# Seven block products for eight in half of the k tiles of two SwiGLU layers' gate and up projections

## The chip, the cores and the metric

The kernel runs on one core of a Trainium2 chip. The metric is the device time of one execution in microseconds (us); the lower, the better. Engines are named as the profile names them: PE is TensorE (PEld its weight loads), DVE is VectorE, ACT is ScalarE, POOL is GpSimd, and SP is the queue from which nearly all DMAs are issued.

## The reference

One decoder layer in float32 on 256 tokens of width 2048: a SwiGLU feed-forward layer at half step, a token mixer, and a second feed-forward layer, each between two RMS norms.

```python
def swiglu(h, w_gate, w_up, w_down):
    return (jax.nn.silu(h @ w_gate) * (h @ w_up)) @ w_down
...
    h = h + 0.5 * rms_norm(swiglu(rms_norm(h, pre1), gate1, up1, down1), post1)
    h = h + rms_norm(hybrid_mixer(rms_norm(h, preM), ...), postM)
    h = h + 0.5 * rms_norm(swiglu(rms_norm(h, pre2), gate2, up2, down2), post2)
```

`w_gate` and `w_up` are 2048 x 5632, `w_down` is 5632 x 2048. The mixer (gated linear attention in four heads, softmax attention in eight) is not changed but for where its constants are loaded.

## The kernel before, in words

**Precision.** Every float32 matmul is made of three matmuls in fp32r: a value is split into a high part (rounded to fp32r) and a low part (the rest), and hi x hi, hi x lo and lo x hi are summed. Activations are split once and kept in `xh` (x, transposed, times the norm's weights: per k tile of 128 rows, 256 columns of high parts and 256 of low parts). The factor 1/rms of each token, `late.rc[t]`, is applied to the product instead of to x.

**Weights.** A weight tile is 128 x 1024: two k tiles of 512 output columns. `order` (L57 to L80) lists all of them in the order of use. `prep` (L86) loads one on SP into one of 4 `raw` buffers, makes `whi` on ACT (L99) and `wlo` on DVE (L100); these have RING = 7 places. `take` and `done` (L118, L126) hand a tile to the matmuls and give it back.

**Up blocks.** `up` (L392) makes 512 of the 5632 columns: `columns` (L274) runs over eight tiles of the gate's weights, then over eight of the up projection's; each tile gives 12 matmuls in `mmt` (L258 to L266: two token tiles of 128, two k tiles, three precision terms), with a slice of `xh` as the stationary tile and 512 columns of the weight tile as the moving one. So a block has 192 matmuls. ACT applies silu to the gate's sums (L399), DVE multiplies by the up sums (L403), and `turned` (L406), a generator whose next piece is run by `step` after each weight tile, transposes the result on PE (L411) and splits it into an `act` tile (L415, L416; four buffers). There are 11 such blocks in each feed-forward layer (FFN 1 and FFN 2).

**Down groups.** `down` (L302) takes two blocks' `act` tiles as k and adds to the four 512-wide column groups of `f`, with the same 12 matmuls per weight tile; the sum is copied (L317) or added (L319) to `f`. Groups and blocks alternate (L427 to L436): four blocks, then a group of 16 tiles and two blocks, and so on. The last group makes the norm's sums as it goes (L333 to L335) and hands over to the next stage.

**PSUM.** `pt` (L190) gives one of four tiles of two banks each, which is all of PSUM.

**Order.** The code is straight-line Python. Buffers are given out and the instructions of each engine are put into a fixed order by the framework's scheduler before the run, by data dependence and program order; so an instruction can run well ahead of its place in the code when its inputs and buffers are free. On the chip each engine then works through its list in order, and waits on semaphores.

**Other loads.** `post_weight` (L184) broadcasts a norm's weights (1 MB) into `wpost` and scales them on ACT (L188); `mixer_constants` (L178) loads the mixer's tables. Both stand in the code between FFN 1's groups. The mixer's low-rank decay weights are one short tile in `order`, spread into ring places with POOL memsets (L104 to L111), and used at L528.

Of the kernel before, what the change touches and what calls it, by code (L numbers as in the profile page):

```python
# [34 lines left out]
RING = 7  # L35
# [7 lines left out]


@with_exitstack
def layer(ctx, tc, xT, x, wn, wpo, cst, msk, bdec, wup, wglr, gu1, dn1, win, wo, gu2, dn2, out):
# [4 lines left out]
    ring = ctx.enter_context(tc.tile_pool(name="ring", bufs=RING))  # L51
# [5 lines left out]
    order = []  # L57

    def plan_down(w, groups):
        n = w.shape[0] // 4  # L60
        for a, b in groups:
            for m in range(4):
                order.extend(w[m * n + i] for i in range(a // 2, b // 2))

    def plan_ffn(gu, dn):
        def up(*blocks):
            for b in blocks:
                order.extend(gu[i] for i in range(b * 16, b * 16 + 16))

        up(0, 1, 2, 3)  # L70
        for g in range(4):
            plan_down(dn, DOWN_FFN[g:g + 1])
            up(*((4, 5), (6, 7), (8, 9), (10,))[g])
        plan_down(dn, DOWN_FFN[4:])

    plan_ffn(gu1, dn1)
    order.extend(win[i] for i in range(24))
    order.append(wglr)
    order.extend(win[i] for i in range(24, 96))
    plan_down(wo, DOWN_MIX)  # L80
    plan_ffn(gu2, dn2)

    ready = []
    used, freed = [0], [0]

    def prep(cuts=1):  # L86
        i = len(ready)
        src = order[i]
        n = src.shape[-1]
        raw = ring.tile([P, 1024], F32, name="raw", bufs=4)  # L90
        w = n // cuts
        for c in range(0, n, w):
            SY.dma_start(raw[:, c:c + w], src[:, c:c + w])
        hi = ring.tile([P, 1024], F32R, name="whi")
        lo = ring.tile([P, 1024], F32R, name="wlo")
        if n == 1024:
            for c in range(0, n, w):
                c = slice(c, c + w)
                A.activation(hi[:, c], raw[:, c], AF.Copy)  # L99
                V.tensor_tensor(lo[:, c], raw[:, c], hi[:, c].bitcast(F32), ALU.subtract)  # L100
            ready.append((hi, lo))
        else:

            r = raw[:, :n].rearrange("p (h k c) -> p h k c", h=2, c=RANK)  # L104
            for half, both in enumerate((hi, lo)):
                nc.gpsimd.memset(both.bitcast(F32), 0.0)
# [6 lines left out]
    def ahead():  # L113

        while len(ready) < min(len(order), freed[0] + RING):
            prep()
# [185 lines left out]
    def down(groups, lhs, fin):  # L302

        ss = [small.tile([P, 4], F32, name="ss%d" % t) for t in range(NT)]
        for g, (a, b) in enumerate(groups):
# [17 lines left out]
            for t in range(NT):  # L323
                for m in range(4):
                    p = pt()[:, t]
                    for i in range(n):
                        if t == 0:
                            slots.append(take())
# [486 lines left out]
```

## Time and profile before

| | us |
|---|---|
| three runs, median | 1931.71 |
| lowest and highest | 1931.46, 1932.37 |
| the profiled execution | 1932.02 |
| its span in the profile | 1930.2 |

The span runs from the first to the last recorded instruction; the profiled execution's own time is 1.8 us longer. Busy times of an engine are the sum of its instructions' durations with overlaps counted once; since matmuls are pipelined, a matmul's own duration (some 393 ns) is longer than the distance between two of them. "Idle before" is the time an engine stood still just ahead of an instruction of that group, and behind the arrow stands what ended it.

### The profile page before, as it was taken

The page shows a single profiled execution, that of the slowest core. Times are in us where ns is not written, and L with a number is a line of the kernel's source. Part 1 is how long each engine was busy: PE and PEld are TensorE (multiplying, and loading weights), DVE is VectorE, ACT ScalarE, POOL GpSimd, SP SyncE. Part 2 cuts the span into 40 slices and gives each one's busy share as a digit, 9 for nine tenths or more (in the row PEclk, how much of TensorE's full clock was granted, in tenths as well). Part 3 has the DMA queues.
Part 4 walks back from the last instruction along what each step waited for, and adds up shares of the span by engine and source line. Part 5 has one row for each costly group of instructions (what it writes and reads, how often), then busy time and mean ns, then how long its engine had stood idle before and what let it go on. Part 6 is the DMA issues. An engine that isn't in the chain of part 4 may idle for free.

```text
span 1930.2 us, 22431 instructions
## 1 busy us (share of the span) xinstructions
PE 1891.8 (98%) x8728; PEld 1562.9 (81%) x8728; DVE 1045.1 (54%) x1141; ACT 884.0 (46%) x1052; POOL 2.0 (0%) x6
## 2 busy tenths in 40 slices
PE   8999999999999998999999998999999999999997
PEld 6888888888888885889888885888888888888885
DVE  5554455545445458468455647544445545545455
ACT  8444444344443436454445547444444344344442
POOL 0000000000000000000000000000000000000000
PEclk9999999999999999999999998999999999999999
DMA  9755555555555554554454554555555555555552
GB/s 326 251 191 188 185 194 185 191 191 185 195 187 186 196 185 142 178 163 144 134 170 159 190 196 133 193 188 190 189 188 193 186 191 186 193 187 189 192 186 87
DMA packets 98650, 356.24 MB, mean 185 GB/s; under 512 B 11088, under 2 KB 11344, under 8 KB 97904
## 3 DMA queue, kind: packets, MB, share of 16 engines
q1 hardware_dynamic: 97968, 353.77, 55.3%
q8 instruction: 68, 1.11, 0.2%
q10 hardware_dynamic: 576, 1.05, 0.2%
q14 instruction: 38, 0.31, 0.0%
HBM read 352.67 MB, written 2.10 MB: 184 GB/s over the span
## 4 chain that ended last, share of the span: by engine, by line
PE 94%; DVE 3%; ACT 1%; DMA 1%; issue 1%; SPq 0%; DVEq 0%; ACTq 0%
PE pt L266 27%; PE pt L264 27%; PE pt L265 27%; PE pt L252 6%; PE pt L253 3%; PE pt L411 1%; DVE wlo L100 1%; PE pt L601 1%; ACT whi L99 1%; DMA raw<-in_gu 0%; DMA h<-in_x 0%; DVE f L335 0%; DVE h L359 0%; DVE f L333 0%; ACT junk L360 0%
## 5 line engine op out<-in xcount | busy, mean ns | idle before, releaser
L100 DVE TENSOR_TENSOR wlo<-raw,whi 128x1024 fp32r<-128x1024 f32 (+1 forms) x657 | 802.9, 1223 | 818.9 <-ACT whi L99 818.0
L99 ACT ACTIVATE whi<-raw 128x1024 fp32r<-128x1024 f32 (+1 forms) x657 | 695.0, 1059 | 962.6 <-PE pt L266 868.9
L264 PE MATMUL pt<-whi,xh 128*128 128x512 f32 x1664 | 654.7, 393 | 11.2 <-ACT whi L99 6.0
L266 PE MATMUL pt<-whi,xh 128*128 128x512 f32 x1664 | 651.5, 392 | 2.1 <-DVE xh L378 2.1
L265 PE MATMUL pt<-wlo,xh 128*128 128x512 f32 x1664 | 650.3, 391 | 0.8 <-DVE wlo L100 0.8
L264 PEld LDWEIGHTS pt<-whi,xh 128*128 128x128 f32 x1664 | 313.7, 189 | 81.6 <-ACT xh L377 11.6
L266 PEld LDWEIGHTS pt<-whi,xh 128*128 128x128 f32 x1664 | 313.7, 189 | 70.1 <-DVE xh L378 5.0
L265 PEld LDWEIGHTS pt<-wlo,xh 128*128 128x128 f32 x1664 | 313.9, 189 | 65.6 <-DVE wlo L100 2.0
L264 PE MATMUL pt<-whi,act 128*128 128x512 f32 x704 | 278.6, 396 | 0.0
L265 PE MATMUL pt<-wlo,act 128*128 128x512 f32 x704 | 277.7, 395 | 0.0
L266 PE MATMUL pt<-whi,act 128*128 128x512 f32 x704 | 277.7, 394 | 0.0
L252 PE MATMUL pt<-xh,whi 128*128 128x512 f32 x512 | 182.0, 399 | 0.0
L266 PEld LDWEIGHTS pt<-whi,act 128*128 128x128 f32 x704 | 132.6, 188 | 30.9
L265 PEld LDWEIGHTS pt<-wlo,act 128*128 128x128 f32 x704 | 132.7, 188 | 30.5
L264 PEld LDWEIGHTS pt<-whi,act 128*128 128x128 f32 x704 | 132.7, 188 | 30.5
L253 PE MATMUL pt<-xh,wlo 128*128 128x256 f32 x512 | 143.6, 281 | 0.0
L252 PEld LDWEIGHTS pt<-xh,whi 128*128 128x128 f32 x512 | 96.1, 188 | 22.7 <-issue 0.8
L253 PEld LDWEIGHTS pt<-xh,wlo 128*128 128x128 f32 x512 | 96.6, 189 | 0.2
L319 DVE TENSOR_TENSOR f<-f,pt 128x1024 f32<-128x1024 f32 x32 | 39.1, 1221 | 20.6 <-PE pt L266 20.6
L403 DVE SCALAR_TENSOR_TENSOR fs<-pt,rs_c,fs 128x512 f32<-128x512 f32 x44 | 31.1, 747 | 10.0 <-PE pt L266 10.0
L399 ACT ACTIVATE fs<-pt,rs_c 128x512 f32<-128x512 f32 x44 | 27.5, 673 | 0.0
L416 DVE TENSOR_TENSOR act<-pt,act 128x1024 fp32r<-128x1024 f32 x22 | 26.8, 1217 | 0.0
(138 smaller groups left out, 529.6 us busy)
## 6 DMA issues: line engine op xcount, KB each, us to landing
raw<-in_gu SPq DMA_DIRECT2D x351, 512.0 KB, 3.3
raw<-in_dn SPq DMA_DIRECT2D x176, 512.0 KB, 3.3
raw<-in_win SPq DMA_DIRECT2D x96, 512.0 KB, 3.3
raw<-in_wo SPq DMA_DIRECT2D x32, 512.0 KB, 3.2
wpost<-in_wpo SPq DMA_DIRECT2D x3, 1024.0 KB, 4.8
hT<-in_xT SPq DMA_DIRECT2D x8, 256.0 KB, 7.1
h<-in_x SPq DMA_DIRECT2D x2, 1024.0 KB, 8.2
out<-h SPq DMA_DIRECT2D x4, 256.0 KB, 2.6
```

The lines of the kernel that those rows point to most:

```text
L99: A.activation(hi[:, c], raw[:, c], AF.Copy)
L100: V.tensor_tensor(lo[:, c], raw[:, c], hi[:, c].bitcast(F32), ALU.subtract)
L252: T.matmul(o, hv[:, k, c], a, start=first and k == 0, stop=False)
L253: T.matmul(o[:, S:], lv[:, k, c], a[:, 0:S], start=False, stop=last and k == 1)
L264: T.matmul(o, hi, hv[:, i], start=first and i == 0, stop=False)
L265: T.matmul(o, hi, lv[:, i], start=False, stop=False)
L266: T.matmul(o, lo, hv[:, i], start=False, stop=last and i == 1)
L319: V.tensor_tensor(f[:, m], f[:, m], p, ALU.add)
L399: A.activation(s[:, t], g2[:, t], AF.Silu, scale=late.rc[t])
L403: V.scalar_tensor_tensor(s[:, t], u2[:, t], late.rc[t], s[:, t], op0=ALU.mult, op1=ALU.mult)
L411: T.transpose(p[:, j // 2, j % 2 * S + t * P:j % 2 * S + (t + 1) * P], s[:, t, j * P:(j + 1) * P], ident)
L416: V.tensor_tensor(a[:, :, S:], src, a[:, :, 0:S].bitcast(F32), ALU.subtract)
```

## The change

In each FFN, block 0 stays as it was. Blocks 1 to 10 become *units*. In a unit, the gate and up projections of 512 columns each are taken together as a 2 x 2 x 2 block product: two token tiles, two halves of k, and two projections. For the first eight of the 16 k tiles this is done by Strassen's algorithm in Winograd's form: four weight tiles W11, W12, W22, W21 (a *quad*; two quads per unit) give seven products with W11, W22, W21 and the sums T1 = W11 + W12, T2 = T1 + W22, T3 = W12 + W22, T4 = T2 + W21. The sums are made on DVE in float32 and split into high and low parts like any weight tile; each of these seven *forms* takes a ring place and is used for six matmuls (one token tile's worth of stationary data, two k tiles, three terms). The other eight weight tiles of a unit are used as before, 12 matmuls each, and add to the same PSUM sums. The unit's order is: quad, four single tiles, quad, four single tiles.

The matching sums of x over token tiles and k halves are made once per FFN (`mixed`, started inside block 0) and kept split in `mix`. As the two token tiles have different 1/rms factors, x of the second tile is scaled by their ratio `rho` (turned into a row by a small matmul) before the sums, and `rho` is applied to the products that need it at the end. Five of the products are combined at the second quad's end (one copy on ACT, four additions on DVE), the rest at the unit's end (four instructions on DVE, one silu of 1024 columns on ACT, one product on DVE). A unit holds all four PSUM tiles.

Around it: RING is 8 instead of 7, and there are 5 `raw` buffers instead of 4. A down group is cut into two halves (two column groups each), and units stand between the halves: block 0, unit 1, unit 2, half, unit 3, half, unit 4, and so on; the last two groups follow unit 10. `act` has 3 buffers instead of 4. `wpost` is no tile of its own any more: in the FFNs it takes the place of `mix` after unit 10, in two loads; in the mixer it takes two of its tiles. The mixer's constants, and the decay weights, are loaded at the start of the mixer into its own pool, which uses the memory of FFN 1's tiles; the decay weights are split by one ACT and one DVE instruction. The squares that went to a `junk` tile go to `f` or to PSUM.

```diff
-RING = 7
+RAW = 5
+RING = 8
+NQ = 2
...
+FFN = [("up", 0, ()), ("up", 1, ()), ("up", 2, ())]
+for _g in range(4):
+    for _i, _ms in enumerate(((0, 1), (2, 3))):
+        FFN += [("down", _g, _ms), ("up", 3 + 2 * _g + _i, ())]
+FFN += [("down", 4, range(4)), ("down", 5, range(4))]
+UNIT = [("q", 0), ("s", 4), ("s", 12), ("s", 5), ("s", 13), ("q", 1), ("s", 6), ("s", 14), ("s", 7), ("s", 15)]
...
+    def plan_quad(w11, w12, w22, w21):
+        forms.extend((kind, len(source)) for kind in ("w11", "t1", "t3", "w22", "t2", "w21", "t4"))
+        source.extend((w11, w12, w22, w21))
...
+    def added(name, a, b):
+        t = sum_pool[0].tile([P, 1024], F32, name=name, tag="sum", bufs=2)
+        V.tensor_tensor(t, a, b, ALU.add)
+        sums.append(t)
...
+        if kind == "w" or kind == "w11":
+            if kind == "w11":
+                added("t1", w[0], w[1])
+            split(w[0], cuts)
+        elif kind == "t1":
+            added("t2", sums[-1], w[2])
+            split(sums[-2])
+        elif kind == "t3":
+            added("t3", w[1], w[2])
+            split(sums[-1])
+        elif kind == "w22":
+            split(w[2])
+        elif kind == "t2":
+            split(sums[-2])
+        elif kind == "w21":
+            V.tensor_tensor(sums[-2], sums[-2], w[3], ALU.add)
+            split(w[3])
        else:
+            split(sums[-2])
...
-                A.activation(junk, c, AF.Square, accum_out=self.hs[t][:, m:m + 1])
+                A.activation(f[:, m, t], c, AF.Square, accum_out=self.hs[t][:, m:m + 1])
...
+            mix = fp.tile([P, 2, 4, 2 * NQ, P], F32R, name="mix", tag="mix")
+            def mixed():
+                while None in late.rc:
+                    yield
+                V.reciprocal(rho, late.rc[0])
+                V.tensor_tensor(rho, rho, late.rc[1], ALU.mult)
+                row = small.tile([P, P], F32, name="rrow", bufs=1)
+                A.activation(row, row_of([rho]), AF.Copy)
+                yield
+                v = f.rearrange("p m t c -> p (m t c)").rearrange("p (k s) -> p k s", s=S)
+                for k in range(0, 4 * NQ, 4):
+                    c = v[:, k:k + 4]
+                    V.tensor_tensor(c, xh[:, k:k + 4, 0:S].bitcast(F32), xh[:, k:k + 4, S:].bitcast(F32), ALU.add)
+                    yield
+                    V.tensor_tensor(c[:, :, P:], c[:, :, P:], row[:, None, :].to_broadcast([P, 4, P]), ALU.mult)
+                    yield
+                k0, k1 = slice(0, 2 * NQ), slice(2 * NQ, 4 * NQ)
+                x11, x12, x21, x22 = v[:, k0, 0:P], v[:, k1, 0:P], v[:, k0, P:], v[:, k1, P:]
+                m = v[:, 4 * NQ:8 * NQ].rearrange("p k s -> p (k s)").rearrange("p (n k s) -> p n k s", n=4, s=P)
+                V.tensor_tensor(m[:, 0], x22, x21, ALU.subtract)
+                V.scalar_tensor_tensor(m[:, 1], m[:, 0], -1.0, x11, op0=ALU.mult, op1=ALU.subtract)
+                yield
+                V.tensor_tensor(m[:, 2], x11, x21, ALU.subtract)
+                V.tensor_tensor(m[:, 3], x12, m[:, 1], ALU.add)
+                for i in range(0, 4, 2):
+                    yield
+                    A.activation(mix[:, 0, i:i + 2], m[:, i:i + 2], AF.Copy)
+                    V.tensor_tensor(mix[:, 1, i:i + 2], m[:, i:i + 2], mix[:, 0, i:i + 2].bitcast(F32), ALU.subtract)
...
+            def product(o, slot, q, lhs, first, last):
+                hv, lv = (x.rearrange("p (k c) -> p k c", k=2) for x in slot)
+                for i in range(2):
+                    a = lhs(2 * q + i)
+                    T.matmul(o, a[:, 0], hv[:, i], start=first and i == 0, stop=False)
+                    T.matmul(o, a[:, 0], lv[:, i], start=False, stop=False)
+                    T.matmul(o, a[:, 1], hv[:, i], start=False, stop=last and i == 1)
+            def unit(b):
+                p16, p57, p23, q4e = pt(), pt(), pt(), pt()
+                into = {"w11": (p16[:, 0], xlhs(0, 0)), "t1": (p57[:, 0], mlhs(0)), "t3": (p57[:, 1], mlhs(2)),
+                        "t2": (p16[:, 1], mlhs(1)), "w22": (p23[:, 1], mlhs(3)), "w21": (p23[:, 0], xlhs(1, 0)),
+                        "t4": (q4e[:, 0], xlhs(1, 1))}
+                s = fp.tile([P, NT, 512], F32, name="fs", bufs=2)
+                u = fp.tile([P, NT, 512], F32, name="fu")
+                nq, ns = 0, 0
+                for kind, i in UNIT:
+                    if kind == "q":
+                        nq += 1
+                        for _ in range(7):
+                            name = forms[used[0]][0]
+                            o, lhs = into[name]
+                            alone = name in ("w11", "t1", "t3", "t2")
+                            product(o, take(), i, lhs, nq == 1, alone and nq == NQ)
+                            done()
+                        if nq == NQ:
+                            A.activation(s[:, 0], p16[:, 0], AF.Copy)
+                            V.tensor_tensor(s[:, 1], p16[:, 1], s[:, 0], ALU.add)
+                            V.tensor_tensor(u[:, 0], p57[:, 0], s[:, 1], ALU.add)
+                            V.tensor_tensor(s[:, 1], p57[:, 1], s[:, 1], ALU.add)
+                            V.tensor_tensor(u[:, 1], p57[:, 1], u[:, 0], ALU.add)
+                    else:
+                        ns += 1
+                        slot = take()
+                        j, k = i // 8, 2 * (i % 8)
+                        end = ns > 2 * (8 - 2 * NQ) - 2
+                        mmt(p23[:, j], 0, slot, (k, k + 1), False, end, xrhs)
+                        mmt(q4e[:, j], 1, slot, (k, k + 1), j == 1 and ns == 2, end, xrhs)
+                        done()
+                        if nq == NQ:
+                            step()
+                V.tensor_tensor(s[:, 0], p23[:, 0], s[:, 0], ALU.add)
+                V.tensor_tensor(u[:, 0], p23[:, 1], u[:, 0], ALU.subtract)
+                V.scalar_tensor_tensor(s[:, 1], q4e[:, 0], rho, s[:, 1], op0=ALU.mult, op1=ALU.add)
+                V.scalar_tensor_tensor(u[:, 1], q4e[:, 1], rho, u[:, 1], op0=ALU.mult, op1=ALU.subtract)
+                A.activation(s, s, AF.Silu, scale=late.rc[0])
+                V.scalar_tensor_tensor(s, u, late.rc[0], s, op0=ALU.mult, op1=ALU.mult)
+                side.append(turned(b, s))
...
-                a = fp.tile([P, 4, 2 * S], F32R, name="act", bufs=4)
+                a = fp.tile([P, 4, 2 * S], F32R, name="act", bufs=3)
...
+            for kind, i, ms in FFN:
+                if kind == "down" and i < 5:
+                    down(DOWN_FFN[i], ms, arhs)
+                elif kind == "down":
+                    down_last(DOWN_FFN[i], arhs, wpost, fin)
+                else:
+                    (up if i == 0 else unit)(i)
+                if kind == "up" and i == 10:
+                    both = fp.tile([P, 2, 4, 2 * NQ, P], F32, name="wpost", tag="mix")
+                    both = both.rearrange("p a b c s -> p (a b c s)")
+                    wpost = [both[:, h * 1024:h * 1024 + 1024].rearrange("p (m c) -> p m c", m=2) for h in range(2)]
+                    for i in range(2):
+                        post_weight(wpost[i], post, scale, i)
...
+        gr = mp.tile([P, KT, RANK], F32, name="gr")
+        gw = mp.tile([P, KT, 2 * RANK], F32R, name="gw")
+        cum, bias = cm[:, 0:128], cm[:, 128:512]
+        SY.dma_start(gr.rearrange("p k c -> p (k c)"), wglr)
+        SY.dma_start(bd, bass.AP(tensor=bdec.tensor, offset=bdec.offset, ap=[[0, P], [1, HG * DK]]))
+        SY.dma_start(wu, wup)
+        SY.dma_start(cm, cst[:, 256:768])
+        SY.dma_start(ms, msk)
...
+        A.activation(gw[:, :, 0:RANK], gr, AF.Copy)
+        V.tensor_tensor(gw[:, :, RANK:], gr, gw[:, :, 0:RANK].bitcast(F32), ALU.subtract)
+        for k in range(KT):
+            T.matmul(p[:2 * RANK], gw[:, k], xh[:, k, :], start=k == 0, stop=k == KT - 1)
```

## Rows read from the trace of the kernel before

**Rows 1.** The page, parts 1 and 2: busy time, and the span in 40 slices.
```profile
PE 1891.8 (98%) x8728; PEld 1562.9 (81%) x8728; DVE 1045.1 (54%) x1141; ACT 884.0 (46%) x1052; POOL 2.0 (0%) x6
...
PEclk9999999999999999999999998999999999999999
```

**Rows 2.** The page, part 4: the chain that ended last, by engine and by line.
```profile
PE 94%; DVE 3%; ACT 1%; DMA 1%; issue 1%; SPq 0%; DVEq 0%; ACTq 0%
PE pt L266 27%; PE pt L264 27%; PE pt L265 27%; PE pt L252 6%; PE pt L253 3%; PE pt L411 1%; DVE wlo L100 1%; PE pt L601 1%; ACT whi L99 1%; DMA raw<-in_gu 0%; DMA h<-in_x 0%; DVE f L335 0%; DVE h L359 0%; DVE f L333 0%; ACT junk L360 0%
```

**Rows 3.** Groups by line: busy us, mean ns | idle us before, releasers.
```profile
L100 DVE TENSOR_TENSOR wlo<-raw,whi 128x1024 fp32r<-128x1024 f32 (+1 forms) x657 | 802.9, 1223 | 818.9 <-ACT whi L99 818.0 <-PE pt L266 0.3
L99 ACT ACTIVATE whi<-raw 128x1024 fp32r<-128x1024 f32 (+1 forms) x657 | 695.0, 1059 | 962.6 <-PE pt L266 868.9 <-PE pt L252 68.5 <-issue 12.3
L264 PE MATMUL pt<-whi,xh 128*128 128x512 f32 x1664 | 654.7, 393 | 11.2 <-ACT whi L99 6.0 <-ACT xh L377 5.2
L266 PE MATMUL pt<-whi,xh 128*128 128x512 f32 x1664 | 651.5, 392 | 2.1 <-DVE xh L378 2.1
L265 PE MATMUL pt<-wlo,xh 128*128 128x512 f32 x1664 | 650.3, 391 | 0.8 <-DVE wlo L100 0.8
...
L264 PE MATMUL pt<-whi,act 128*128 128x512 f32 x704 | 278.6, 396 | 0.0
...
L319 DVE TENSOR_TENSOR f<-f,pt 128x1024 f32<-128x1024 f32 x32 | 39.1, 1221 | 20.6 <-PE pt L266 20.6
L403 DVE SCALAR_TENSOR_TENSOR fs<-pt,rs_c,fs 128x512 f32<-128x512 f32 x44 | 31.1, 747 | 10.0 <-PE pt L266 10.0
L399 ACT ACTIVATE fs<-pt,rs_c 128x512 f32<-128x512 f32 x44 | 27.5, 673 | 0.0
L416 DVE TENSOR_TENSOR act<-pt,act 128x1024 fp32r<-128x1024 f32 x22 | 26.8, 1217 | 0.0
...
L272 DVE TENSOR_TENSOR bt<-pt,tb 128x512 f32<-128x512 f32 x16 | 11.0, 686 | 3.1 <-ACT tb L271 3.1
...
L736 DVE TENSOR_TENSOR go<-go,g 128x1024 f32<-128x1024 f32 x1 | 1.2, 1224 | 1.3 <-ACT g L510 1.3
```

**Rows 4.** The chain in order of time: start us, us, what; the blocks' transposes.
```profile
58.60 0.87 PE pt L411 x8
103.01 0.87 PE pt L411 x8
147.44 0.88 PE pt L411 x8
192.00 0.87 PE pt L411 x8
280.86 0.87 PE pt L411 x8
```

**Rows 5.** Timeline of PE around one block's transposes: start us, us, instruction.
```profile
102.85 1.03 PE L411 MATMUL pt<-cs,fs 128*128 128x128 f32 x8
103.64 0.48 PE L264 MATMUL pt<-whi,xh 128*128 128x512 f32 x1
```

**Rows 6.** Timeline of DVE in three stretches: start us, us, instruction [idle before].
```profile
39.64 0.16 DVE L202 SCALAR_TENSOR_TENSOR rs_c<-rs_a,rs_r 128x1 f32<-128x1 f32 x1
...
53.20 0.75 DVE L403 SCALAR_TENSOR_TENSOR fs<-pt,rs_c,fs 128x512 f32<-128x512 f32 x1 [1.49 <-PE pt L266]
53.86 1.22 DVE L100 TENSOR_TENSOR wlo<-raw,whi 128x1024 fp32r<-128x1024 f32 x1
54.99 0.74 DVE L403 SCALAR_TENSOR_TENSOR fs<-pt,rs_c,fs 128x512 f32<-128x512 f32 x1
55.66 3.49 DVE L100 TENSOR_TENSOR wlo<-raw,whi 128x1024 fp32r<-128x1024 f32 x3
...
97.61 1.41 DVE L403 SCALAR_TENSOR_TENSOR fs<-pt,rs_c,fs 128x512 f32<-128x512 f32 x2 [0.40 <-PE pt L266]
...
487.63 1.22 DVE L319 TENSOR_TENSOR f<-f,pt 128x1024 f32<-128x1024 f32 x1 [0.47 <-PE pt L266]
488.77 1.22 DVE L100 TENSOR_TENSOR wlo<-raw,whi 128x1024 fp32r<-128x1024 f32 x1
```

**Rows 7.** Timeline of SP, 26 to 46 us: issue us, us, DMA.
```profile
28.95 0.87 SPq L186 DMA_DIRECT2D wpost<-in_wpo  x1
...
38.47 0.69 SPq L179 DMA_DIRECT2D cm<-in_cst  x1
```

**Rows 8.** Windows: stretch, its us, busy by engine, PEclk, DMA share, GB/s.
```profile
12.00:34.00 22.00, 21.97 (x96) 17.85 (x96) 15.02 (x27) 18.80 (x33) 0.00 (x0) 1.00 1.01 405
34.00:58.40 24.40, 24.36 (x107) 20.15 (x108) 16.73 (x21) 18.81 (x23) 0.00 (x0) 1.00 0.84 286
```

**Rows 9.** The page, part 6: DMA issues, KB each, us to landing.
```profile
raw<-in_gu SPq DMA_DIRECT2D x351, 512.0 KB, 3.3
...
wpost<-in_wpo SPq DMA_DIRECT2D x3, 1024.0 KB, 4.8
```

**Rows 10.** Timeline of ACT, 40 to 50 us.
```profile
44.62 2.94 ACT L99 ACTIVATE whi<-raw 128x1024 fp32r<-128x1024 f32 x3
```

More of the change, by code (lines that the diff above doesn't have):

```diff
@@ L54, in layer @@
     ps = ctx.enter_context(tc.tile_pool(name="ps", bufs=4, space=PSUM))
[L57 to L74 removed]
+    source, forms = [], []
@@ L84, in layer, with load @@
[L84 to L90, printed above, removed]
+    raws, ready, sums = [], [], []
+    read, used, freed = [0], [0], [0]
+    sum_pool = [None]
+    def load(cuts=1):
+        i = len(raws)
+        n = source[i].shape[-1]
+        raw = ring.tile([P, 1024], F32, name="raw", bufs=RAW)
         w = n // cuts
         for c in range(0, n, w):
[L93 to L101, printed above, removed]
-        else:
-            r = raw[:, :n].rearrange("p (h k c) -> p h k c", h=2, c=RANK)
-            for half, both in enumerate((hi, lo)):
-                nc.gpsimd.memset(both.bitcast(F32), 0.0)
-                v = both.rearrange("p (k c) -> p k c", c=P)
-                h_, l_ = v[:, :, 0:RANK], v[:, :, RANK:2 * RANK]
-                A.activation(h_, r[:, half], AF.Copy)
-                V.tensor_tensor(l_, r[:, half], h_.bitcast(F32), ALU.subtract)
-            ready.append((hi, lo))
@@ L113, in ahead, with split @@
-    def ahead():
-        while len(ready) < min(len(order), freed[0] + RING):
-            prep()
+            SY.dma_start(raw[:, c:c + w], source[i][:, c:c + w])
+        raws.append(raw)
+    def split(w, cuts=1):
+        hi = ring.tile([P, 1024], F32R, name="whi", bufs=RING)
+        lo = ring.tile([P, 1024], F32R, name="wlo", bufs=RING)
+        n = 1024 // cuts
+        for c in range(0, 1024, n):
+            c = slice(c, c + n)
+            A.activation(hi[:, c], w[:, c], AF.Copy)
+            V.tensor_tensor(lo[:, c], w[:, c], hi[:, c].bitcast(F32), ALU.subtract)
+        ready.append((hi, lo))
@@ L118, in take @@
+    def ahead():
+        more = True
+        while more:
+            more = False
+            while len(raws) < min(len(source), read[0] + RAW):
+                load()
+            if can_prep():
+                prep()
+                more = True
     def take():
@@ new lines, in layer, with down @@
+    ss = [small.tile([P, 4], F32, name="ss%d" % t) for t in range(NT)]
+    def down(g, ms, lhs):
+        a, b = g
+        n = (b - a) // 2
+        for m in ms:
+            p = pt()
+            for i in range(n):
+                slot = take()
+                for t in range(NT):
+                    mmt(p[:, t], t, slot, (a + 2 * i, a + 2 * i + 1), i == 0, i == n - 1, lhs)
+                done()
+                step()
+            if a == 0:
+                A.activation(f[:, m], p, AF.Copy)
+            else:
+                V.tensor_tensor(f[:, m], f[:, m], p, ALU.add)
```

158 lines of the change are left out of this document (85 added, 73 removed).

## The prediction

> **What bounds the kernel now.** I read the busy shares first: TensorE (PE) is busy for 1891.8 of 1930.2 us, VectorE (DVE) for 1045.1 and ScalarE (ACT) for 884.0, and the granted clock stands at full speed in all but one of the 40 slices [rows 1]. A busy PE need not be the bound, so the chain of waits comes next: 94% of it is PE, and 81% is three lines, L264 to L266, the matmuls of `mmt` [rows 2]. The groups by line then say whether those wait: the xh ones waited 14.1 us in all (11.2, 2.1 and 0.8), the act ones not at all [rows 3]. So the time is the number of matmuls times their pace, and work for DVE and ACT is free as long as it is ready in time.
>
> The pace is not the 393 ns of a row, since matmuls overlap. The chain in order of time has the eight transposes of each block at 58.60, 103.01, 147.44 and 192.00 [rows 4]. Between the first two lie one up block (192 matmuls) and eight transposes: 44.41 us. The PE timeline has such eight from 102.85 to the next matmul at 103.64, 0.79 us [rows 5], so 43.62 us / 192 = 0.2272 us a matmul. From 192.00 to 280.86 lie 216 matmuls of xh, 168 of act and eight transposes [rows 4]: 88.86 - 0.79 - 49.07 = 39.0 us, 0.232 us for one with `act` as its stationary tile.
>
> **What is removed.** A quad takes four weight tiles of 12 matmuls (48) and makes seven products of six (42). A unit has two quads, 12 matmuls fewer, and each FFN has ten units (block 0 stays): 2 x 10 x 12 = 240 matmuls. 240 x 0.2272 = **54.5 us**, all on the path. Nothing else of PE's work changes but two small matmuls for `rho`'s row. The profiled execution took 1932.0 us against a median of 1931.7, so its time serves for both: 1932.0 - 54.5 = **1877.5**.
>
> **What is added on DVE**, for one unit, by durations in [rows 3]: 22 splits for 16, 22 x 1.223 = 26.9; eight weight sums of 1024 columns, like L736, 8 x 1.22 = 9.8; the combining at the second quad's end, 4 x 0.686 = 2.7 (L272 reads PSUM at 512 columns), and at the unit's end 2 x 0.686 + 2 x 0.747 + 1.22 = 4.1; `turned`'s subtraction 1.22. That is 44.7 us, against 22.3 now. The half down group that follows has eight splits and two adds to f, 12.2 us. Cover: PE needs 180 x 0.2272 = 40.9 for the unit and 96 x 0.232 + 0.79 = 23.1 for the half group. So **DVE has 56.9 us of work in a cycle of 64.0 (89%), where it had 34.5 in 66.7 (52%)**. ACT gets six splits more (6.4 us), a copy (0.6) and one silu of 1024 columns (about 1.05) for two of 0.673: some 35 us of 64. Both hide, on average.
>
> Within a cycle DVE is uneven. A quad costs it eleven instructions, 13.4 us, while PE spends 42 x 0.2272 = 9.5 on it; four single tiles cost 4.9 against 10.9. Quad plus four singles: 18.3 against 20.4 us. Eight ring places carry this: when PE starts a quad, its seven forms and one more can be ready, and the last form is needed only 8.2 us later, so DVE may be 6 us late before PE feels it. Tightest is the start of each FFN, units 1 and 2 with no down work between: 89.4 us of DVE for 83.4 of PE.
>
> Here a rule is weighed. Three splits back to back take 3.49 us, so a further one costs (3.49 - 1.22) / 2 = 1.135 us, not 1.223 [rows 6]; at that rate the some forty long instructions of a cycle come to 3.5 us less, 53.4 of 64.0, and units 1 and 2 to about 84 of 83.4. The Trainium skill, VectorE: DVE Perf Modes, Terms, says the next instruction cannot issue until the pipe has emptied (DRAIN); by that 56.9 would be a floor. The trace disagrees: neighbours overlap by 0.09 us. The sum is the same either way, only the third rival's chance moves.
>
> **Where a wait can appear.** (a) *Transposes after a unit.* Now they follow 24 matmuls of the next work, 5.24 us after the block's last result (97.61 in the DVE timeline, transposes at 102.85), and their input is ready at 99.02 [rows 5, 6]. Afterwards the input is late by a chain: two adds and one scaled add, 1.9 us, silu 1.05, the product 1.22, about 4.3; with one split of 1.14 between them, since a freed ring place asks for one, 5.4. Bounds: 0 and 1.0 us per unit (a second split); I take 0.2, **+4 us** for 20 units, near the row with one split. What is late next is that block's act tile, used only a group later. (b) *The mixes of x.* They need `rc`, which in FFN 1 is complete at 39.80; block 0 ends at about 53.2, where its first L403 starts [rows 6], and unit 1's second product, the first to read a mix, is due 1.4 us later. In these 14.8 us DVE has 8 us for the mixes (two 1024-wide adds, two 512-wide products, four sums, two splits), and, ahead of them in the program, seven splits as now, four weight sums and block 0's two products, 14: 22 in all. Bounds 0 (the mixes slip between) and 8; I take half, **+4**. In FFN 2 a block of 43 us covers them. (c) *Pace with `mix` as stationary tile.* xh gives 0.2272, act 0.232; 48 such matmuls a unit: 0 to 20 x 48 x 0.0048 = 4.6 us. I take 0, as the moving tile and the rest are those of the xh row, and keep 4.6 for the range. (d) *Queues.* On SP the bytes are the same; the broadcasts leave the first 60 us (issued at 28.95 and 38.47 now [rows 7], while the DMA engines are saturated [rows 8]). Behind unit 10 two of them wait for `mix`, with weight loads behind them: 13 tiles (eight ring places, five raw buffers) of 2.73 us, 35 us of PE, are issued by then, and a landing takes 4.8 us [rows 9]. ACT's scaling of them waits for the landing with splits behind it, covered by eight ring places, 21 us. The mixer's five constant loads wait until FFN 1's tiles are free, under the same 13 tiles; the decay weights' split, two short instructions, replaces a ring place and POOL's memsets. All this I cost at nothing, up to 3 us for the mixer. PE is saturated from 12 to 58 us already [rows 8], so the lighter start gives at most 1 us back.
>
> Sum: 1877.5 + 4 + 4 = 1885.5, **forecast 1885**; bounds 1876.5 (none of a to c, 1 us back) to 1913 (20 + 8 + 4.6 + 3).
>
> **Rivals.** *First, transposes at full price:* as (a), with two or more splits in the way, 1 to 1.5 us per unit, 20 to 30: with (b) 1902 to 1912. For: preps stand ahead in the program, and L100 already slips between two L403 [rows 6]. Against: the queues are not in program order (L319 runs before the split issued ahead of it [rows 6]), so late transposes may be put further back.
>
> *Second, PSUM.* A unit takes all four PSUM tiles. If its first product waits until the group before has been added to f, PE loses L319's 1.22 us, or 2.4 with a split ahead of it, at 16 units behind half groups: 20 to 38 us, with (b) 1902 to 1920. Against: the code first touches the tile that comes free last in the seventh product, 8 us on, and no matmul row shows a PSUM wait [rows 3]. The Trainium skill, Perfetto Trace Analysis, Identifying the Most-Contended Engine, says a gap that repeats on the engine that should be saturated can mean too few buffers for the next tile; this trace has no such gap.
>
> *Third, DVE becomes the bound, and the kernel slower.* DVE waits for ACT's high part before nearly every split: 818.0 us over 657 [rows 3]. If that handover (1.06 us) is not overlapped in the 14 quad forms, and the silu is waited for too, DVE's cycle is 56.9 + 14 x 1.06 + 1 = 72.8, 8.8 over PE's 64.0: net 6.1 lost per unit, 1932 + 122 = 2054. It decides from 9.8 us of such waits per cycle (66.7 - 56.9), about nine of the fourteen. Against: under backlog ACT runs ahead (three splits in 2.94 us [rows 10]) and DVE packs three in 3.49 [rows 6].
>
> *Fourth, nothing:* products and waits cancel at 2.7 us per unit, 1928 to 1936.
>
> **How the numbers follow.** Forecast 0.62, first rival 0.16, second 0.10, third 0.09, fourth 0.03. Three runs spread by 0.05%, and 0.2% (3.9 us) is about what can be told from no change. Faster: the forecast and the first two rivals, 0.88; same 0.03; slower 0.09. The range runs from 1874, a little under the lower bound, to 1909: it holds the forecast but for all its bad bounds together, most of the first rival and a part of the second; the rest of these, the third and the fourth are outside, some 0.2.
>
> **What would show it.** Right: 240 matmuls fewer; PE about 41 us from a unit's first product to its last; DVE near 1500 us busy with hardly a PE wait named after it; transposes with under 0.5 us ahead of them. First rival: idle time before the transposes, released by the product of gate and up. Second: idle time at a unit's first products, released by the add to f. Third: waits on the low parts of quad forms, DVE at nine tenths or more across the FFNs. The forecast is wrong if the units' matmul pace differs from 0.227, or if PE idles over 1 us per unit.

## The result, and the profile after

The changed kernel takes **1909.76 us** (median of 4 runs, 1907.85 to 1911.94) against 1931.59 before: a ratio of 0.9887 (95% interval 0.9869 to 0.9904). It is faster by 21.8 us, not by the 46.7 forecast, and ends 0.8 us above the range. The profiled execution took 1907.85 us, its span is 1906.1, so the profiled spans differ by 24.1 us. That is set against the 54.5 us that 240 matmuls would give: **30.4 us are missing** there. The profiled execution is the fastest of the four; by the medians 32.7 us are missing.

The page of the kernel after, parts 1, 2 and 4:

```profile
PE 1850.9 (97%) x8492; PEld 1517.9 (80%) x8492; DVE 1469.2 (77%) x1584; ACT 1010.2 (53%) x1177; POOL 0.2 (0%) x4
...
PEclk9899999999999998999999998999999999999999
...
PE 75%; DVE 12%; DMA 7%; issue 3%; ACT 2%; SPq 0%; DVEq 0%; ACTq 0%
```

The matmuls are gone as counted (8728 to 8492 with the few small ones that are new) and DVE stands at 1469.2 us, near the 1500 forecast. But the chain has changed its character: PE's share fell from 94% [rows 2] to 75%, and DVE and DMA took 19%. The clock row has two slices more under nine tenths: the one from 47.7 us holds the long wait below, the one from 714.8 the entry of the mixer, which ends FFN 1 with the clock at 0.79 as it did before (0.72).

Which waits these are is in the groups by line (busy us, mean ns | idle us before, releasers):

```profile
L493 PE MATMUL pt<-whi,mix 128*128 128x512 f32 x320 | 127.8, 399 | 9.3 <-ACT mix L479 9.3
L136 DVE TENSOR_TENSOR t<-raw 128x1024 f32<-128x1024 f32 x80 | 97.7, 1221 | 34.3 <-DMA raw<-in_gu 33.3
L495 PE MATMUL pt<-whi,xh 128*128 128x512 f32 x240 | 93.8, 391 | 0.0
L562 PE MATMUL pt<-cs,fs 128*128 128x128 f32 x176 | 23.5, 277 | 8.2 <-DVE fs L537 8.0
```

PE waits at two new places: 9.3 us, once, for the mixes of x, and 8.2 us in all for the product of gate and up ahead of the transposes. DVE itself waits 33.3 us for landings ahead of the weight sums (L136). And the record of a matmul on `mix` is 8 ns longer than that of one on xh in the same quads (399 against 391); experiments 9 to 13 measure the distance between their starts.

**The one long wait.** The PE timeline where the first quad of FFN 1 reaches its first mix, and windows of that stretch (us, busy by engine, PEclk, DMA share, GB/s):

```profile
53.30 0.39 PE L495 MATMUL pt<-whi,xh 128*128 128x512 f32 x1
62.96 0.80 PE L493 MATMUL pt<-whi,mix 128*128 128x512 f32 x1 [9.27 <-ACT mix L479]
```

```profile
45.00:53.30 8.30, 8.30 (x39) 6.86 (x38) 5.66 (x9) 2.35 (x4) 0.00 (x0) 1.00 0.24 76
53.30:62.96 9.66, 0.39 (x2) 0.00 (x1) 9.66 (x11) 6.61 (x8) 0.00 (x0) 0.71 0.46 156
62.96:67.50 4.54, 4.54 (x10) 3.15 (x11) 4.54 (x5) 1.39 (x2) 0.00 (x0) 0.50 0.33 115
```

DVE is busy for all of the 9.66 us, and once PE starts again its granted clock is 0.50, the level of 1.2 GHz, for ten matmuls. This quad takes 21.43 us (52.17 to 73.60), a later one 9.69 (1457.15 to 1466.84), so 11.7 us are lost here: 9.4 while PE stands, and most of the rest with the ten matmuls at half the clock, which take 4.54 us. One part of the cause goes back to SP's queue, of before and then of after (issue us, us, DMA):

```profile
12.35 3.95 SPq L93 DMA_DIRECT2D raw<-in_gu  x3
16.36 0.42 SPq L458 DMA_DIRECT2D h<-in_x  x1
```

```profile
12.12 13.24 SPq L121 DMA_DIRECT2D raw<-in_gu  x9
25.41 0.43 SPq L611 DMA_DIRECT2D h<-in_x  x1
```

SP has nine weight loads to issue there instead of three before it comes to x, and most of them wait for room. The rearrangement does this, not the products: without Strassen (experiment 7) x is issued at 25.71, and with a sixth landing tile (experiment 5) at 25.32, behind ten loads. So `rc` is complete at 44.02 instead of 39.80. The other part is DVE's own queue: it waits for rho's row at the end of that chain, and then the mixes stand among the splits and weight sums of block 0 and unit 1 (timeline of DVE):

```profile
43.86 0.16 DVE L255 SCALAR_TENSOR_TENSOR rs_c<-rs_a,rs_r 128x1 f32<-128x1 f32 x1
...
46.20 0.15 DVE L458 TENSOR_TENSOR rho<-rho,rs_c 128x1 f32<-128x1 f32 x1
46.27 1.22 DVE L131 TENSOR_TENSOR wlo<-t,whi 128x1024 fp32r<-128x1024 f32 x1
50.13 0.69 DVE L467 TENSOR_TENSOR f<-f,rrow 128x512 f32<-128x512 f32 x1 [2.64 <-ACT rrow L460]
...
65.37 1.21 DVE L480 TENSOR_TENSOR mix<-f,mix 128x1024 fp32r<-128x1024 f32 x1
```

Between `rc` and ACT's first high part of a mix (61.87) lie 17.9 us. DVE stands still for 2.64 of them and spends 11.4 on ten weight sums and splits (1.14 us from one to the next).

**The short waits.** One seam between a unit and the next group, on DVE and then on PE:

```profile
1498.12 1.23 DVE L136 TENSOR_TENSOR t<-raw 128x1024 f32<-128x1024 f32 x1 [2.75 <-DMA raw<-in_gu]
1499.26 1.22 DVE L131 TENSOR_TENSOR wlo<-raw,whi 128x1024 fp32r<-128x1024 f32 x1
1500.39 0.68 DVE L532 TENSOR_TENSOR fs<-pt,fs 128x512 f32<-128x512 f32 x1
1500.99 1.22 DVE L131 TENSOR_TENSOR wlo<-raw,whi 128x1024 fp32r<-128x1024 f32 x1
1502.13 0.68 DVE L533 TENSOR_TENSOR fu<-pt,fu 128x512 f32<-128x512 f32 x1
1502.73 0.74 DVE L534 SCALAR_TENSOR_TENSOR fs<-pt,rho,fs 128x512 f32<-128x512 f32 x1
1503.39 0.74 DVE L535 SCALAR_TENSOR_TENSOR fu<-pt,rho,fu 128x512 f32<-128x512 f32 x1
1504.04 1.21 DVE L131 TENSOR_TENSOR wlo<-raw,whi 128x1024 fp32r<-128x1024 f32 x1
1505.18 1.28 DVE L537 SCALAR_TENSOR_TENSOR fs<-fu,rs_c,fs 128x1024 f32<-128x1024 f32 x1
```

```profile
1506.51 1.09 PE L562 MATMUL pt<-cs,fs 128*128 128x128 f32 x8 [0.84 <-DVE fs L537]
```

The unit's last matmul starts at 1498.06, but its combining does not begin until 1500.39: a weight sum stands ahead of it and waits 2.75 us for its load. Two more splits stand within it. The product is done at 1506.46, and the transposes, put 31 matmuls behind the unit, have waited 0.84 us. Such waits stand at 14 of the 22 blocks. The row's 8.2 us understate them: a row counts idle time from the end of the matmul before, 0.39 us after its start, where the next would have started after 0.23. From matmul start to transpose start the 22 seams take 15.6 us, and 5.1 in the kernel before, so they cost 10.5.

### The profile page after: what moved, and what is told of

Its sections match the earlier page's. It is cut to its first block, busy times and chain, and to the rows that moved or that the text cites. A ratio compares the mean times of both kernels' runs of the same rounds, so it can differ in the third digit from the quotient of the medians.

```text
span 1906.1 us, 22667 instructions
## 1 busy us (share of the span) xinstructions
PE 1850.9 (97%) x8492; PEld 1517.9 (80%) x8492; DVE 1469.2 (77%) x1584; ACT 1010.2 (53%) x1177; POOL 0.2 (0%) x4
## 4 chain that ended last, share of the span: by engine, by line
PE 75%; DVE 12%; DMA 7%; issue 3%; ACT 2%; SPq 0%; DVEq 0%; ACTq 0%
PE pt L319 16%; PE pt L318 16%; PE pt L317 16%; DVE wlo L131 6%; PE pt L305 6%; PE pt L493 5%; PE pt L495 5%; PE pt L494 5%; DMA raw<-in_gu 3%; DMA raw<-in_dn 3%; PE pt L306 3%; ACT whi L130 2%; PE pt L562 1%; DVE fs L537 1%; PE pt L768 1%
## 5 line engine op out<-in xcount | busy, mean ns | idle before, releaser
L131 DVE TENSOR_TENSOR wlo<-raw,whi 128x1024 fp32r<-128x1024 f32 (+1 forms) x617 | 750.4, 1220 | 247.7 <-ACT whi L130 243.5
L317 PE MATMUL pt<-whi,xh 128*128 128x512 f32 x1024 | 404.7, 395 | 9.0 <-ACT whi L130 6.1
L319 PE MATMUL pt<-whi,xh 128*128 128x512 f32 x1024 | 402.5, 393 | 5.7 <-DVE xh L435 5.7
L318 PE MATMUL pt<-wlo,xh 128*128 128x512 f32 x1024 | 401.3, 392 | 0.1
L130 ACT ACTIVATE whi<-t 128x1024 fp32r<-128x1024 f32 x160 | 169.2, 1058 | 289.8 <-DVE t L136 116.9
L131 DVE TENSOR_TENSOR wlo<-t,whi 128x1024 fp32r<-128x1024 f32 x160 | 195.5, 1222 | 90.6 <-ACT whi L130 90.4
L317 PEld LDWEIGHTS pt<-whi,xh 128*128 128x128 f32 x1024 | 193.5, 189 | 53.3 <-ACT xh L434 8.0
L319 PEld LDWEIGHTS pt<-whi,xh 128*128 128x128 f32 x1024 | 193.3, 189 | 50.4 <-DVE xh L435 10.1
L318 PEld LDWEIGHTS pt<-wlo,xh 128*128 128x128 f32 x1024 | 193.8, 189 | 39.8 <-DVE wlo L131 0.9
L318 PEld LDWEIGHTS pt<-wlo,act 128*128 128x128 f32 x704 | 132.6, 188 | 30.2
L493 PE MATMUL pt<-whi,mix 128*128 128x512 f32 x320 | 127.8, 399 | 9.3 <-ACT mix L479 9.3
L494 PE MATMUL pt<-wlo,mix 128*128 128x512 f32 x320 | 127.2, 397 | 0.0
L495 PE MATMUL pt<-whi,mix 128*128 128x512 f32 x320 | 126.7, 397 | 0.0
L136 DVE TENSOR_TENSOR t<-raw 128x1024 f32<-128x1024 f32 x80 | 97.7, 1221 | 34.3 <-DMA raw<-in_gu 33.3
```

The costliest lines, as they stand in the source:

```text
L130: A.activation(hi[:, c], w[:, c], AF.Copy)
L131: V.tensor_tensor(lo[:, c], w[:, c], hi[:, c].bitcast(F32), ALU.subtract)
L136: V.tensor_tensor(t, a, b, ALU.add)
L317: T.matmul(o, hi, hv[:, i], start=first and i == 0, stop=False)
L318: T.matmul(o, hi, lv[:, i], start=False, stop=False)
L319: T.matmul(o, lo, hv[:, i], start=False, stop=last and i == 1)
```

## The experiments

Each was measured beside the kernel before, whose median was then 1931.4 to 1931.8 us; ratios are to it, with 95% intervals. Diffs are against the changed kernel (in experiment 13 against the kernel before) and show their main lines only.

**1. Block 1 of FFN 1 without Strassen.**

```
-                    (up if i == 0 else unit)(i)
+                    (up if i < (2 if first else 1) else unit)(i)
```

> Block 1 of FFN 1 stays plain (16 tiles, no quads), so the mixes are read one block later; 12 matmuls come back. Theory M, the first unit of FFN 1 waits for the mixes of x (21.4 us for a quad that takes 9.7 elsewhere): 11.7 us go, 2.5 us come back, about 1900.5. Rival D, the wait is DVE's backlog of weight sums and splits at the first quad, wherever that quad stands: the wait moves to unit 2, about 1912.

1901.71 us, 0.9844 (0.9828 to 0.9861). Faster by 8.1 us although one unit less saves 12 matmuls, 2.7 us, less; the wait for a mix is gone. So having unit 1 so early cost some 10.8 us. (The plan of loads changes likewise; the mixes are still made behind block 0, at 58.48 to 63.37, with x as late as before.) The wait did not move to unit 2, as the rival had it; but a plain block 1 also takes unit 1's weight sums and extra splits off DVE, so the run does not tell the mixes from that work.

**2. x loaded right behind the constants,** ahead of those nine weight loads.

```
+        for t in range(NT):
+            SY.dma_start(h[:, t], x[t * P:(t + 1) * P, :])
...
-        for t in range(NT):
-            SY.dma_start(h[:, t], x[t * P:(t + 1) * P, :])
-            yield
```

> The two loads of x for FFN 1's norm are issued ahead of the ninth weight load instead of behind nine more; nothing else. Theory M-late, the mixes in FFN 1 are late because x and so the token factors are late (complete at 44.0 us against 39.8 before the change): the mixes come some 8 us sooner, the wait of 11.7 falls to about 5, about 1903 to 1905. Rival D, behind it stands DVE's own backlog at units 1 and 2 (7.6 us lost there without any mixes): at most 4 us go, 1906 to 1909.

1905.27 us, 0.9864 (0.9849 to 0.9879), between the two forecasts. `rc` is complete at 30.94, 13.1 us sooner, and the first quad takes 9.70 us. That does not show late x to be the cause of the wait, for the mixes hardly come sooner (timeline of DVE):

```profile
40.50 3.50 DVE L131 TENSOR_TENSOR wlo<-raw,whi 128x1024 fp32r<-128x1024 f32 x3 [2.53 <-ACT whi L130]
43.91 0.69 DVE L467 TENSOR_TENSOR f<-f,rrow 128x512 f32<-128x512 f32 x1
...
63.83 1.22 DVE L480 TENSOR_TENSOR mix<-f,mix 128x1024 fp32r<-128x1024 f32 x1
```

The last part of a mix begins 1.5 us sooner (63.83 for 65.37), ACT's first 2.9 us sooner (58.94 for 61.87). The quad does not wait because it starts 7.15 us later, at 59.32 instead of 52.17: the weights that now land behind x come late for block 0:

```profile
26.32 0.49 PE L317 MATMUL pt<-whi,xh 128*128 128x512 f32 x1 [3.13 <-ACT whi L130]
27.91 0.79 PE L318 MATMUL pt<-wlo,xh 128*128 128x512 f32 x1 [1.09 <-DVE wlo L131]
```

Most of what was won goes there. The DMA engines are near full from 12 to 34 us (share 1.00 in the changed kernel, 0.93 here), so what one load gains there others lose. How soon the mixes would come with both x and the weights in time, no run shows.

**3. The mixes are not made;** the products read slices of xh instead.

```
-                return lambda k: mix[:, :, i, k]
+                return xlhs(i % 2, i // 2)
```

> The mixes of x are not made, and the four products that read them read slices of xh instead, so the gate and up values are other numbers; matmuls, weight sums and splits stay. Theory M and the pace of matmuls with mix as stationary tile (0.234 against 0.227 us): 11.7 us and 20 x 0.25 = 5 us go, about 1893. Rival D (backlog of weight work): the pace's 5 us go and at least half of the wait stays, 1899 to 1905.

1900.33 us, 0.9843 (0.9829 to 0.9858), in the range of rival D. The quads run at xh's pace (9.52 us), but units 1 and 2 lose 6.5 us to weight tiles and act tiles that are late (1.4 in unit 1, and unit 2's first quad takes 14.69):

```profile
98.29 0.50 PE L471 MATMUL pt<-wlo,xh 128*128 128x512 f32 x1 [0.98 <-DVE wlo L131]
101.69 0.50 PE L470 MATMUL pt<-whi,xh 128*128 128x512 f32 x1 [1.98 <-DVE act L544]
```

So the start of FFN 1, which the prediction called tightest, is bound by DVE for a moment even without the mixes; in the changed kernel the wait for the mixes gives DVE the time to catch up.

**4. The transposes one weight tile later.**

```
             def turned(b, s):
                 yield
+                if b < 10:
+                    yield
```

> The transposes of units 1 to 9 stand one weight tile further back in the program; nothing else. Theories R and S alike: PE no longer stands before them, 8 to 10.5 us go, about 1900. If the seam's cost is not the transposes but DVE's lateness as such, the wait turns up a few matmuls later and the time stays at 1909.

1897.58 us, 0.9826 (0.9811 to 0.9841): 12.2 us less than the changed kernel, and the wait is gone:

```profile
L564 PE MATMUL pt<-cs,fs 128*128 128x128 f32 x176 | 23.0, 273 | 0.1
```

Between the profiled executions it is 10.4 us, and the seams, counted from start to start, fall from 15.6 to 5.5 us, 10.1 less; the rest of the 12.2 is that the profiled execution of the changed kernel was 1.9 us below its median. The transposes now stand 36 matmuls behind the unit there, not 31.

**5. Six landing tiles instead of five** (two tables of the mixer and one temporary share room for it).

```
-RAW = 5
+RAW = 6
```

> Six raw buffers instead of five (room from the mixer: the decay weights' tiles share its lv buffers, tb has one buffer); nothing else. Theory R, the wait before the transposes comes from a weight sum that waits for a late load (2.75 us in the unit looked at) and stands ahead of the combining in DVE's queue: the seams' 10.5 us go, about 1899. Rival S, the combining is simply longer than the matmuls in front of the transposes: unchanged, 1908 to 1911.

1904.01 us, 0.9857 (0.9843 to 0.9872), 5.8 us less, about half of what the first theory wanted. The sums now hardly wait for loads, and the transposes wait half as long:

```profile
L136 DVE TENSOR_TENSOR t<-raw 128x1024 f32<-128x1024 f32 x80 | 97.8, 1223 | 5.9 <-DMA raw<-in_gu 4.5
L562 PE MATMUL pt<-cs,fs 128*128 128x128 f32 x176 | 23.6, 277 | 4.3 <-DVE fs L537 4.2
```

The first quad takes nearly as long as in the changed kernel (20.97 us). So the late loads make some two fifths to a half of the seam (from start to start 10.5 us become 6.7); what is left goes to the chain of combining, silu, product and the splits among it.

**6. The first weight sum one form later.**

```
-            if kind == "w11":
-                added("t1", w[0], w[1])
             split(w[0], cuts)
...
+            added("t1", w[0], w[1])
             added("t2", sums[-1], w[2])
```

> The changed kernel, but the weight sum of the first form, which needs a late load, is made after the split of the first block instead of ahead of it; loads and everything else are as before. Theory L (the transposes come late because the sum waits for its load at the head of VectorE's queue, ahead of the combining): the waits of the transposes fall from 10.5 us to 3 to 5, and the time to 1902 to 1905. Rival C (they come late because the chain of combining, activation and product itself is too long for the seven matmuls left to it): unchanged, 1907 to 1912, waits 9 to 11.

1911.75 us, 0.9894 (0.9877 to 0.991): no change, and 9.5 us of waits. It does not decide between the two, since the sum still came first. At the same seam:

```profile
1503.14 1.22 DVE L136 TENSOR_TENSOR t<-raw 128x1024 f32<-128x1024 f32 x1 [2.57 <-DMA raw<-in_gu]
1504.28 1.22 DVE L131 TENSOR_TENSOR wlo<-raw,whi 128x1024 fp32r<-128x1024 f32 x1
1505.42 0.68 DVE L531 TENSOR_TENSOR fs<-pt,fs 128x512 f32<-128x512 f32 x1
```

**7. No Strassen at all,** everything rearranged as in the change (plans, landing tiles, order of the FFN).

```
-                    (up if i == 0 else unit)(i)
+                    up(i)
```

> All blocks are plain again (16 tiles, 192 matmuls), no sums; what stays are the halved down groups, eight ring places, five raw and three act buffers, and the moved constants and post weights. Theory: these cost some 2 us (mixer entry 1.1, end 0.9), 1932 to 1935. Rival: the rearrangement costs a good part of the missing 30 us itself, 1940 or more.

1932.74 us, 1.0003 (0.9994 to 1.0013). The rearrangement by itself costs some 1 us, and by the interval at most 2.5.

**8. The two remedies together** (1 and 4).

> Transposes one tile later and FFN 1's block 1 plain, together. If the two waits are separate their gains add: 1909.8 - 12.2 - 8.1, about 1889.5. If DVE's lateness is one wait that only changes its place, less than that: 1893 or more.

1888.10 us, 0.9775 (0.976 to 0.979): they add up.

**9. The pace: the ring at the other end of SBUF.**

```
-    ring = ctx.enter_context(tc.tile_pool(name="ring", bufs=1))
+    ring = ctx.enter_context(tc.tile_pool(name="ring", bufs=1, side="right"))
```

> The pool of weight buffers is laid at the other end of SBUF, so that act and mix lie at lower addresses; no instruction is added or removed. Theory A, where the stationary tile lies sets the pace (xh 0.227 us a matmul, act and mix 0.233): 2112 matmuls of act and 960 of mix gain 0.006 each, 18 us, about 1891. Rival B, it is something else about these tiles: unchanged, 1908 to 1911. Theory A with the moving tile's address counting as well: the pace of xh changes too.

1928.62 us, 0.998 (0.997 to 0.9989). Not one instruction differs, and 18.9 us are lost: matmuls on xh are now 0.2334 us apart like the others. The theory fell, but the place of the tiles decides something.

**10. Landing and combining tiles at the other end,** so that all operands of the products lie low.

```
-        raw = ring.tile([P, 1024], F32, name="raw", bufs=RAW)
+        raw = far.tile([P, 1024], F32, name="raw", bufs=RAW)
```

(and `h`, `f`, `fs`, `fu` likewise; `far` is a pool with side="right")

> The changed kernel, but the landing tiles of the weights, h, f and the combining's tiles lie at the other end of SBUF, so that the split weights, xh, the mixes and the activations lie close together at the lower end. No instruction is changed. Theory P (a matmul has the faster pace only if both of its operands lie at the lower end): mixes and activations take xh's pace, 0.2268 us instead of 0.2325, over 2112 matmuls of the activations and 960 of the mixes some 17 us: 1890 to 1895. Rival Q (the pace hangs on something else, such as the traffic beside it): unchanged, 1907 to 1912, with mixes and activations still at 0.232 to 0.234. A third outcome, as in the kernel that had the split weights at the other end, is that xh becomes slow as well: about 1928.

1911.61 us, 0.9895 (0.9881 to 0.991): unchanged, and mixes and activations are as slow as before. Neither end nor distance is it. The addresses in the programs suggest another rule. Where the tiles begin, in bytes past a multiple of 256, and the mean distance of matmul starts in ns, over all stretches of at least 24 matmuls without a wait (from the PE timeline):

```
kernel            whi/wlo  xh   mix  act    pace on xh  on mix  on act
before              128    128   -    0       226.7       -      232.4
after               128    128   0    0       226.9     232.7    232.6
ring at the right   224    128   0    0       233.4     233.4    233.3
tiles moved (10)    128    128   0    0       227.0     232.8    232.7
```

The fast pairs lie alike. Four more kernels test that, and whether the cost, some 17 us, belongs to the change at all.

**11. A gap ahead of the FFN's tiles,** so that mixes and activations begin at 128 as well.

```
             fp = es.enter_context(tc.tile_pool(name="ffn", bufs=1))
+            fp.tile([P, 480], F32, name="gap")
```

> The changed kernel with an unused tile of 1920 bytes a partition ahead of the FFN's tiles, so that mixes and activations begin 128 bytes past a multiple of 256 as the split weights and xh do. No instruction is changed. Theory A (a matmul has the faster pace if both of its operands lie alike modulo 256): mixes and activations come down to xh's 0.2268 us, some 2112 x 0.0058 + 960 x 0.0055 = 17.5 us: 1890 to 1895. Rival Q (the pace goes with what the tiles hold, or with who writes them): unchanged, 1907 to 1912.

1895.85 us, 0.9816 (0.9801 to 0.9831). 13.9 us less, just above the range, and 226.7 to 226.9 ns on xh, mixes and activations alike. The groups by line:

```profile
L318 PE MATMUL pt<-wlo,act 128*128 128x512 f32 x704 | 275.2, 391 | 0.0
L494 PE MATMUL pt<-whi,mix 128*128 128x512 f32 x320 | 126.1, 394 | 9.3 <-ACT mix L480 9.3
...
L563 PE MATMUL pt<-cs,fs 128*128 128x128 f32 x176 | 23.6, 277 | 13.1 <-DVE fs L538 13.1
```

The seams take back a part: with PE faster, the transposes wait 13.1 us, 4.9 more than in the changed kernel. That more than covers the gap between 13.9 and the 17.5 expected.

**12. The same, with all tiles 128 bytes further on,** so that all four begin at 0.

```
+    const.tile([P, 32], F32, name="gap0")
     eps = const.tile([P, 1], F32, name="eps")
...
+            fp.tile([P, 480], F32, name="gap")
```

> As pad, and another unused tile of 128 bytes ahead of everything, so that split weights, xh, mixes and activations all begin on a multiple of 256. Theory A, of one operand against the other: as pad, 1890 to 1895. Theory B (what counts is that the stationary operand, or the moving one, begins 128 bytes past a multiple of 256): all matmuls at 0.2325 to 0.2335, about 1925 to 1930. Rival Q: 1907 to 1912.

1898.36 us, 0.9834 (0.9818 to 0.9851), with 226.7 to 226.9 ns on all three. The time is 3.4 us above the range; the transposes wait 14.1 us here. The pace is what the run was for: 128 and 0 are equally good, and what counts is that the two operands lie alike.

```profile
L319 PE MATMUL pt<-wlo,act 128*128 128x512 f32 x704 | 275.2, 391 | 0.0
```

**13. A gap in the kernel before.**

```
             fp = es.enter_context(tc.tile_pool(name="ffn", bufs=1))
+            fp.tile([P, 96], F32, name="gap")
```

> The kernel before with an unused tile ahead of the FFN's tiles, so that its activations begin 128 bytes past a multiple of 256, as its split weights and xh do. Theory A: 2112 x 0.0056 = 12 us less than the kernel before, 1918 to 1921. Rival Q: unchanged, 1931 to 1932.

1920.62 us, 0.9942 (0.9927 to 0.9957), 226.8 on activations. So most of that cost is older than the change, and 10.8 us can be had without it.

```profile
L264 PE MATMUL pt<-whi,act 128*128 128x512 f32 x704 | 274.9, 390 | 0.0
```

**14. All three remedies** (1, 4 and 11).

> The kernel with later transposes and FFN 1's block 1 plain (1888.1 us), with the unused tile of 1920 bytes. Theory A: 1888.1 less 2112 x 0.0058 and 912 x 0.0055 us: 1869 to 1874. Rival Q: 1886 to 1891.

**1873.63 us**, 0.9699 (0.9685 to 0.9713), the fastest of all, 36.1 us below the changed kernel. Against the kernel before with the same gap (1920.62) it is 47.0 us faster for 228 matmuls less, which by count are worth 228 x 0.2268 = 51.7.

## Why the prediction was wrong

**What held.** The count and the pace of a unit: two quads of 9.69 and twice four single tiles of 10.88 make 41.1 us, forecast 40.9. DVE's load, 1469.2 for about 1500. The queues and the rearrangement, 0 to 3, were 1.0 (experiment 7). So the matmuls are worth what they were said to be; the failure lies in what they were to be paid with. The two terms priced at 4 us each were some three times as large, and one taken at 0 was not. From the profiled executions alone 11.7 (mixes) + 10.5 (transposes) + 5.6 to 6.8 (pace) + 1.2 (rearrangement) = 29.0 to 30.2 of the 30.4 us that are missing there; by the medians (10.8 to 11.7, 12.2, 5.6 to 6.8, 1.0) 29.6 to 31.7 of 32.7. The result lies within the prediction's own sum of bad bounds, 1913, which its range cut off at 1909.

**Step (b), the wait for the mixes, was mis-sized: 4 priced, bounds 0 to 8, 11.7 measured.** It failed at two points. It took `rc` at 39.80, where the trace of before has it; the change moves it to 44.02, because the load of x is issued 9.05 us later behind six more weight loads. The prediction says of SP's queue that the bytes are the same, and looked only at the broadcasts, not at x. And it took half of its bound, as if the mixes would slip between the weight work. They did not: after `rc`, ten weight sums and splits (11.4 us) and 2.64 us of standing still for rho's row, which passes through PE and ACT, come before the first part of a mix. PE, left without work for 9.3 us, then runs ten more matmuls at a granted clock of 0.50, which the step did not count. The second point weighs more as far as the runs show: with `rc` 13.1 us sooner the mixes came only 1.5 to 2.9 us sooner (experiment 2, where late weights held DVE up as well), and without any mixes units 1 and 2 still lost 6.5 us (experiment 3). A block of time more for DVE gives 10.8 us back (experiment 1). How the 11.7 us divide between late x and DVE's work stays open.

**Step (a), the transposes, was mis-sized: 4 us priced, 10.5 measured in the profile and 12.2 by the medians of experiment 4.** The step counted adds, silu, product and one split, 5.4 us, against 24 matmuls, 5.24. In the seam shown, the transposes stand behind 31 matmuls (7.2 us), and the product is still late, for it comes 8.0 us after the end of the last matmul. Two splits stand within the chain. And the step left out that the weight sum of the next quad stands ahead of the combining and waits for a landing: no row of the kernel before has DVE waiting for a landing, since there the load of a split reaches ACT first. The trace of after has 33.3 us of such waits, and some two fifths to a half of the cost goes with them (experiment 5). The first rival had this mechanism, its sign (idle time released by the product of gate and up) and, with 1902 to 1912, the time. The time was luck: it put 20 to 30 us at the transposes and 4 at the mixes.

The Trainium skill, Perfetto Trace Analysis, Optimization Strategy (the section in which the rule weighed by the prediction stands), says that a gap that repeats on the engine that should be saturated can mean too few buffers. Here it bears, though not on PSUM as the prediction weighed it: with a sixth landing tile the repeating gap ahead of the transposes goes from 8.2 to 4.3 us.

**Step (c), the pace on the mixes, was taken at 0 for the wrong reason.** It was taken at 0 because the moving tile is that of the xh row, and 0 to 4.6 were kept for the range; measured are 960 x (232.7 - 226.9) ns = 5.6 us, or 6.8 by 40 quads of 9.69 us where a quad with both tiles alike takes 9.52 (experiment 11). The pace that the prediction read off the `act` rows, 0.232, was no property of the down products but of where their tiles begin.

**The other rivals.** PSUM: no matmul row waits for the add to f. DVE the bound: not over a cycle, 77% of the span; but at the start of FFN 1 it is, busy for all of the long wait, and without the mixes it is still late in units 1 and 2 (experiment 3).

What stays open besides: the rest of the seam, how much of it is the splits within the combining and how much the chain itself, was not taken apart.

## What to carry to other kernels

When a change takes work off the bounding engine and pays with work elsewhere, price the start of each phase and each seam by itself, and date every input anew: here the rearrangement put nine weight loads instead of three ahead of the one that the new work needs. Work that is to slip between other work on an in-order queue should be priced as if it did not. A step that waits for a load at the head of an in-order queue holds up everything behind it, so put sums over several loads where their loads have landed. And where two rows of the same matmul differ by some ns with no wait, compare the addresses of their operands before calling it a property of the work.

## What was not expected of the hardware

A matmul's pace depended on how its stationary and its moving tile lie to one another: 226.7 to 227.0 ns on average where both begin alike modulo 256 bytes, 232.4 to 233.4 where they do not (offsets of 128, 96 and 224 between them). Whether both begin at 128 or both at 0 made no difference. All fast pairs here are also alike modulo 512; which of the two moduli it is was not tried, and why the chip does this no trace shows. An unused tile of 384 bytes a partition was worth 10.8 us in the kernel before, where activations came 5.6 ns a matmul faster. And after an idle stretch of 9.3 us PE ran ten matmuls, 4.5 us, at a granted clock of 0.50.
